# More projection steps ahead of the first head's scores, a pair of heads loaded in one round, and tiles of the mixture loaded two ahead

## The chip, the cores and the metric

The kernel runs on one NeuronCore of a Trainium2 chip. Its engines are TensorE (PE in the profile; PEld is its weight load), VectorE (DVE), ScalarE (ACT), GpSimd (POOL) and SyncE (SP). SP computes nothing here; it issues nearly all DMAs. The metric is the device time of one execution in microseconds (us). A kernel is run several times and the median is given; one further execution is recorded by the hardware profiler.

## The reference

One layer of an encoder, applied with the same weights to two token sets: A with 1024 tokens and B with 512, 1024 channels each. Cut to what matters:

```python
h = rms_norm(x, pre_w)
cols = h @ w_in                                  # about 10,800 columns
m_qk, m_v, m_o, m_z, m_i, m_f, a_qkv, a_z, gate = split(cols)
# branch A, bidirectional mLSTM, 4 heads x 256: q and k by a short conv + SiLU;
# per direction  h_t = (C_t q_t) / max(|n_t . q_t|, 1), gates from m_i and m_f
y_m = headnorm(h_fwd + h_bwd) * sigmoid(m_o) * silu(m_z)
# branch B, attention in 3 groups (window, dilation) = (128,1), (512,4), (2048,16),
# 8 heads x 64 each; the three outputs are mixed by their softmax denominators
o_g = softmax_unnormalised(q_g k_g^T + bias_g) v_g,  with row max m_g and denominator d_g
w_g = exp(m_g - max_g m_g)
y_a = (sum_g w_g o_g) / (sum_g w_g d_g) * silu(a_z)
merged = sigmoid(gate_0) * (y_m @ w_proj_m) + sigmoid(gate_1) * (y_a @ w_proj_a)
out = x + rms_norm(merged @ w_out, post_w)
```

All of it is float32. A dense product is made of three matmuls on a high and a low part of each operand (`mm3`, L190 to L196: high x high, high x low, low x high).

## The kernel before

**The first half** of the span projects the values of both token sets and then the remaining columns of A (`unit_pair`), ending with A's merge gates. **The second half**, from about 1056 us on, is what the change touches. It runs A's mLSTM, A's attention, B's mLSTM, B's attention and the closing products, in this order. Beside each of these stages TensorE is fed with *projection steps*: the projection of B's columns, and later the products with `w_proj_m`, `w_proj_a` and `w_out`.

**Steps and units.** `Fill` holds a list of units. A unit of B's projection makes 128 columns for 512 tokens; it is 8 steps, one for each 128 input channels, and a step is one `mm3`, three matmuls of 128x512. A unit needs one weight tile of 128x1024 (512 KB). The tile is loaded into one of two raw buffers (`wraw`), and `split_w` makes a high part (ACT, L252) and a low part (DVE, L253) into one of three pairs `wh`, `wl` (five pairs from B's attention on). Two tiles are loaded and split before the second half begins. When a unit is begun, `Fill.weights` calls `load`, which has the tile two units further on split (four units further on from B's attention on), and so has its DMA issued if it hasn't been. So the DMA of the third tile stands in the program at the begin of the first unit, the fourth at the begin of the second, the fifth at the begin of the third; the fifth uses the raw buffer of the third.

**Rate.** `fill.stage(steps, shares)` sets how many steps go with one share: A's mLSTM has 210 steps for `lead + 64 + 2 + 4` shares. `fill(lead)` is called before anything of the first head is computed; each of 64 rounds (4 heads x 8 chunks x 2 directions) calls `fill(1/3)` two or three times between its products.

**The order.** In the second half the instructions of TensorE and of SP stand in the order of the program; those of ACT, DVE and POOL are ordered at build time by a scheduler with a timing model. Each of these engines executes its own list in order, so an instruction that waits holds all behind it. SP's DMAs use eight semaphores in turn: a DMA is issued once the one eight before it has landed.

**The start of A's mLSTM** (`mlstm`). SP issues Q and K of the first head, the gate rows `rw`, then V0a and V0b, then whatever `fill(lead)` asks for. `prepare(0)` then computes the scores of the first head (L892) and turns K (L901), with a `fill(1/3)` after each of six parts; `front` builds the decayed scores of a round (`rm`, POOL L924, from `rw`), and `core` makes the products `num` and `kv`.

**B's attention** (`attend`, `attention`, `att_load`). Twelve pairs of heads, four tiles for each pair; a tile goes through `products` (`lg`, L1387), `softmax` (DVE L1399, ACT L1403), `turn` (`pt`, L1410, and its copy `pts`, L1413) and `output` (`o`, L1422), one stage a round, with one share of steps before `output`. At the second tile of a pair the loads of the next pair are queued: for the pair 1, twelve loads of 64 rows of 2 KB (Q and V1a) and two of the bias. `spread(r)` sets how many of the queued loads `tick` issues in a round: the queue's length divided by r, rounded up. `need` issues what is left when the pair begins. In the same rounds SP also loads the weight tiles `wraw<-w_pm`, and rows of `ym_a` (`ymr`, `sraw`) for the product with `w_proj_m`, which ACT splits at L1603.

**The mixtures** (`combine`). For each 128 tokens a tile `cs` of three loads (`og`, 528 bytes a row and pair of heads) is weighed (L1522 to L1533), mixed (L1541), added (L1547) and turned. There are two `cs` tiles. A's mixture runs as a generator beside B's mLSTM (`slow`, a part in each half round); B's runs after B's attention, beside steps of the closing products. `final` makes the closing product with `w_out`, in slots, and writes the result; its DVE instructions are L1711, L1716 and L1719.

Of the kernel before, what the change touches and what calls it, by code (L numbers as in the profile page):

```python
# [175 lines left out]
class Net:  # L176
# [1255 lines left out]
    def attend(self, T, fill, steps, first, banks, outs, after=None, beside=None, at=()):  # L1432

        nc = self.nc
        self.lag = 3 if T.n > 4 else 2
        with ExitStack() as st:
            ps = self.pool(st, "at_ps" + T.name, 2, "right", PSUM)
            sb = self.pool(st, "at" + T.name, 2, "right")  # L1440
            shape = {"lg": [P, 2, 256], "pt": [P, 4, P], "o": [P, 4, P]}
            make = lambda b: ps.tile(shape[b], F32, name=b, bufs=1 if b == "o" and T.n <= 4 else 2)
            spare = {b: make(b) for b in banks}
            self.bank = lambda b: spare.pop(b) if b in spare else make(b)
            bias = self.bias
            self.ot = Rot(self, [sb.tile([P, OW], F32, name=f"ot{i}", bufs=1) for i in range(outs)])
            tiles = []
            fill.stage(steps, 12 * T.n)

            self.xo_end = fill.done + steps  # L1450
            if T.n <= 4:
                self.third, self.fill = lambda: ps.tile([P, BLK], F32, name="dense3", bufs=1), fill

            def ready(u):
                nonlocal bias
                if u == 4 and T.n <= 4:
                    b = [x[F32] for x in bias.bufs]
                    bias = Rot(self, [b[i][:, c:c + 256].bitcast(F32R) for i in range(2) for c in (0, 256)])
                    self.xo_bufs.insert(0, ("stage", b[2:]))
                return self.attention(T, u, first if u == 0 else self.att_load(T, u), bias, sb, ps)  # L1460

            self.later = {}
            coming = ready(0)
            self.need(("table", 0))
            for i in range(12):
                now = coming
                for j, t in enumerate(now):
                    if j == 1:
                        if i < 11:
                            coming = ready(i + 1)  # L1470
                            self.spread(T.n - 1)
                        elif after:
                            after()
                            self.spread(T.n + 1)
                    self.tick()
                    if j == 0:
                        self.need(("att", i))
                    if j == 1:
                        self.need(("table", i))
                        self.later.pop(i, lambda: None)()  # L1480
                    tiles.append(t)
                    self.att_round(tiles, fill)
                    if len(tiles) in at:
                        next(beside, None)
            for _ in range(3):
                self.tick()
                tiles.append(None)
                self.att_round(tiles, fill)
            self.flush(lambda p: True)
            self.third = None  # L1490
            if T.n <= 4:
                self.xo_bufs = [x for x in self.xo_bufs if x[0] != "stage"]
# [10 lines left out]
    def combine(self, T, bank, cs, ys, sb, azs, slow):  # L1503

        nc = self.nc
        cs = [self.take(x, F32)[:, :12 * OW].rearrange("p (g a w) -> p g a w", g=3, a=4) for x in cs]
        ys = [self.take(x, F32) for x in ys]
        az_of = Rot(self, azs + [y[:, 1536:2048] for y in ys])  # L1510

        def load(t):
            for g in range(3):
                self.fetch(("og", T.S), cs[t % 2][:, g], T.og[g, :, t * P:(t + 1) * P].rearrange("h t w -> t h w"))

        by = lambda x: x.rearrange("p g (a b) -> p g a b", a=4)

        def weigh(t):
            c = cs[t % 2]
            w = sb.tile([P, 4, 8], F32, name="cw8", bufs=2)  # L1520
            den, mx = c[:, :, :, 128:130], c[:, :, :, 130:132]
            top = by(w[:, 3:4])[:, 0]  # L1522
            nc.vector.tensor_tensor(top, mx[:, 0], mx[:, 1], op=OP.max)
            nc.vector.tensor_tensor(top, top, mx[:, 2], op=OP.max)
            nc.vector.tensor_sub(by(w[:, :3]), mx, top[:, None].to_broadcast([P, 3, 4, 2]))
            nc.scalar.activation(w[:, :3], w[:, :3], AF.Exp)
            wd = sb.tile([P, 3, 8], F32, name="wd8", bufs=2)
            nc.vector.tensor_tensor(by(wd), by(w[:, :3]), den, op=OP.mult)
            nc.vector.tensor_add(wd[:, 0], wd[:, 0], wd[:, 1])
            nc.vector.tensor_add(wd[:, 0], wd[:, 0], wd[:, 2])  # L1530
            nc.vector.reciprocal(wd[:, 1], wd[:, 0])

            nc.vector.scalar_tensor_tensor(w[:, :3], w[:, :3], 0.5, wd[:, 1][:, None, :].to_broadcast([P, 3, 8]), op0=OP.mult,  # L1533
                                           op1=OP.mult)
            return w[:, :3]

        def mix(t, w):
            c = cs[t % 2]
            y = ys[t % 2][:, :1536].rearrange("p (g a w) -> p g a w", g=3, a=4)
            for g in range(3):  # L1540
                nc.vector.tensor_tensor(y[:, g].rearrange("p a (b e) -> p a b e", e=64),  # L1541
                                        c[:, g, :, :128].rearrange("p a (b e) -> p a b e", e=64),
                                        by(w)[:, g][:, :, :, None].to_broadcast([P, 4, 2, 64]), op=OP.mult)

        def add(t):
            y = ys[t % 2][:, :1536].rearrange("p (g x) -> p g x", g=3)
            nc.vector.tensor_add(y[:, 0], y[:, 0], y[:, 1])  # L1547
            nc.vector.tensor_add(y[:, 0], y[:, 0], y[:, 2])

        def turn(t, az):  # L1550
            p = bank()
            for ct in range(4):
                nc.tensor.transpose(p[:, ct], ys[t % 2][:, ct * P:(ct + 1) * P], self.ident)
            ya = az.rearrange("p (c s) -> p c s", c=4)
            nc.vector.tensor_mul(ya, p, ya)
            self.put(("ym", T.S, 4), T.ym[8:12, :, t * P:(t + 1) * P].rearrange("c p s -> p c s"), ya, az)

        load(0)
        yield
        az, w = {}, []  # L1560
        for t in range(T.n):
            az[t] = az_of()
            self.fetch(("az", T.S), az[t].rearrange("p (c s) -> p c s", c=4), T.az[:, :, t * P:(t + 1) * P].rearrange("c p s -> p c s"))
            if t + 1 < T.n:
                load(t + 1)
            for step in (lambda: w.append(weigh(t)), lambda: mix(t, w[t]), lambda: add(t)):
                with self.tc.issue_after(self.splits[0].ins), self.tc.issue_after(self.splits[1].ins):
                    step()
                if slow:
                    yield  # L1570
            if not slow:
                yield
                yield
            if t > 0:
                turn(t - 1, az[t - 1])
            yield
        yield
        if not slow:
            yield
        turn(T.n - 1, az[T.n - 1])  # L1580
        self.mixed.add(T)
        yield
# [172 lines left out]
STEPS = (210, 202, 164, 290, 86)  # L1755


def body(tc, a):
    N = Net(tc, a)
    nc = tc.nc  # L1760
    (x1, y1), (x2, y2) = a["runs"]
    with ExitStack() as st:
# [4 lines left out]
        A = Tokens(dram, 1024, a[x1], a[y1], "a")  # L1767
# [7 lines left out]
        with ExitStack() as s1:  # L1775
# [4 lines left out]
            with ExitStack() as sv:  # L1780
# [39 lines left out]
                def load(j, k):  # L1820
                    if k < 4:
                        hi, lo, w = HB[j][0][:, k], HB[j][1][:, k], N.prew[:, 4 * j + k:4 * j + k + 1]
                        nc.scalar.activation(hi, xb[j][:, k], AF.Copy, scale=w)
                        nc.vector.scalar_tensor_tensor(lo, xb[j][:, k], w, hi.bitcast(F32), op0=OP.mult, op1=OP.subtract)
                    elif k == 4:
                        for kh in range(2):
                            weights(1, kh)
                        scale(0)
                    else:
                        scale(1)  # L1830
                        inputs(0)
# [123 lines left out]
        with ExitStack() as s1:  # L1955
# [14 lines left out]
            fill = Fill(N, units)  # L1970
# [21 lines left out]
            with ExitStack() as s2:  # L1992
# [2 lines left out]
                sraw = sp.tile([P, BLK + 2], F32R, name="sraw")  # L1995
                N.sg, N.sraw = Rot(N, [sraw[:, :BLK]]), sraw.bitcast(F32)
                head = N.ml_load(A, 0)
                N.mlstm(A, fill, STEPS[0], head, ("a", "num", "kv"), 4,
                        hold("qkv", lambda: N.att_first(A)))
                with ExitStack() as s3:  # L2000
                    lanes = N.lanes_short(B, N.pool(s3, "lane2", 1, "right"), lambda: N.bank("o").rearrange("p a b -> p (a b)"))
# [96 lines left out]
```

## Time and profile before

| what | value |
|---|---|
| median of 3 runs | 2278.14 us (2277.72 to 2280.95) |
| the profiled execution | 2278.09 us, of which the span of the profile 2276.3 us |
| busy share of the span: PE, PEld, DVE, ACT, POOL | 98%, 86%, 64%, 48%, 27% |
| DMA, mean over the span | 187 GB/s, 425.05 MB |
| mean granted TensorE clock | 0.995 |

The span runs from the first to the last instruction of the program in the profile; the time of the execution is 1.8 us longer. Idle time of an engine is given with what ended it. A row of the timeline has the start, the duration, the engine and line, the tiles (out<-in), the shape and count, and in brackets the engine's idle time just before and its releaser. A row of the table by stretches has the stretch, its length, the busy time of PE, PEld, DVE, ACT and POOL with their counts, then the granted clock of TensorE, the busy share of the DMA engines, and GB/s.

### The profile page before, as it was taken

Reading aid. Unit: us, or ns where it says so; the run is one execution under the profiler, and the core shown is the slowest. Engines: PE = TensorE matmul, PEld = TensorE weight load, DVE = VectorE, ACT = ScalarE, POOL = GpSimd, SP = SyncE. Lnnn points to the kernel's source line nnn. Section 1 sums busy time; section 2 is a strip of 40 time slices with the busy share of each in tenths; the row PEclk is TensorE's granted clock in tenths of the full one; section 3 lists DMA queues with packets and bytes.
Section 4 is the critical chain, followed back from the end, with each engine's and each line's share of the span. In section 5 each row is a group of like instructions: output and inputs, shape, how many; then the busy total and the mean of one; then the engine's idle time right before and its main releaser. Section 6 shows DMA issues by size and latency. Waiting matters only on the chain. (4 is left out here: it accounts for less than half of the span.)

```text
span 2276.3 us, 35152 instructions
## 1 busy us (share of the span) xinstructions
PE 2235.5 (98%) x12210; PEld 1951.7 (86%) x12210; DVE 1467.8 (64%) x2777; ACT 1100.5 (48%) x2255; POOL 623.6 (27%) x801
## 2 busy tenths in 40 slices
PE   9999999999999999999999999999999999999998
PEld 9999998888887888887888889989888878888787
DVE  5587556767899655643787776675477744556563
ACT  7444223434444433334677766676644354544332
POOL 1000023333333322222567640001033321311311
PEclk9999999999999999999999999999999999999999
DMA  9556435555332223424666559988788888787673
GB/s 355 192 138 143 117 113 194 196 193 195 118 111 101 95 82 109 146 97 159 242 214 218 157 164 250 237 234 216 203 240 264 250 259 221 192 261 208 219 248 116
DMA packets 253627, 425.05 MB, mean 187 GB/s; under 512 B 26209, under 2 KB 150753, under 8 KB 252681
## 3 DMA queue, kind: packets, MB, share of 16 engines
q1 hardware_dynamic: 249848, 410.20, 58.7%
q10 hardware_dynamic: 3600, 12.59, 1.4%
q8 instruction: 97, 1.59, 0.3%
q14 instruction: 82, 0.66, 0.1%
HBM read 302.72 MB, written 128.37 MB: 189 GB/s over the span
## 5 line engine op out<-in xcount | busy, mean ns | idle before, releaser
L194 PE MATMUL dense<-H,wh 128*128 128x512 f32 x672 | 280.5, 417 | 0.0
L196 PE MATMUL dense<-H,wl 128*128 128x512 f32 x672 | 265.6, 395 | 0.5 <-DVE wl L253 0.5
L195 PE MATMUL dense<-H,wh 128*128 128x512 f32 x672 | 264.5, 394 | 0.0
L196 PE MATMUL d<-Hh,phla 128*128 128x512 f32 x608 | 237.4, 390 | 2.2 <-DVE phla L538 2.2
L194 PE MATMUL d<-Hh,phla 128*128 128x512 f32 x608 | 236.9, 390 | 0.0
L195 PE MATMUL d<-Hl,phla 128*128 128x512 f32 x608 | 236.8, 390 | 0.0
L195 PE MATMUL d<-vlo,Hh 128*128 128x322 f32 x704 | 220.4, 313 | 0.8 <-DVE vlo L384 0.8
L196 PE MATMUL d<-vhi,Hl 128*128 128x322 f32 x704 | 220.3, 313 | 0.0
L194 PE MATMUL d<-vhi,Hh 128*128 128x322 f32 x704 | 220.3, 313 | 0.0
L253 DVE TENSOR_TENSOR wl<-wraw,wh 128x1024 fp32r<-128x1024 f32 x109 | 137.0, 1257 | 89.8 <-ACT wh L252 87.7
L556 POOL TENSOR_TENSOR psum_w<-pw_raw 128x512 f32<-128x512 f32 x38 | 57.5, 1512 | 445.8 <-DMA pw_raw<-w_in 422.1
L1399 DVE CUSTOM_DVE_ANT_0 ls<-lg,bias 128x256 f32<-128x256 f32 (+1 forms) x288 | 93.7, 362 | 132.7 <-PE lg L1387 68.2
L194 PE MATMUL d<-Hh,phlb 128*128 128x512 f32 x456 | 177.6, 390 | 0.0
L196 PE MATMUL d<-Hh,phlb 128*128 128x512 f32 x456 | 177.6, 389 | 0.0
L195 PE MATMUL d<-Hl,phlb 128*128 128x512 f32 x456 | 177.6, 389 | 0.0
L1403 ACT ACTIVATE ls<-ls,nm 128x256 f32<-128x256 f32 (+1 forms) x288 | 129.9, 453 | 79.6 <-DVE nm L1401 63.1
L252 ACT ACTIVATE wh<-wraw 128x1024 fp32r<-128x1024 f32 x110 | 116.0, 1054 | 85.1 <-DMA wraw<-w_pm 32.8
L196 PEld LDWEIGHTS dense<-H,wl 128*128 128x128 f32 x672 | 126.7, 189 | 29.7 <-DVE wl L253 0.9
L195 PEld LDWEIGHTS dense<-H,wh 128*128 128x128 f32 x672 | 127.8, 190 | 13.6
L194 PEld LDWEIGHTS dense<-H,wh 128*128 128x128 f32 x672 | 127.4, 190 | 13.5
L196 PEld LDWEIGHTS d<-Hh,phla 128*128 128x128 f32 x608 | 114.1, 188 | 27.6 <-DVE phla L538 4.2
L195 PEld LDWEIGHTS d<-vlo,Hh 128*128 128x128 f32 x704 | 133.5, 190 | 1.5 <-DVE vlo L384 1.4
(556 smaller groups left out, 5722.2 us busy)
## 6 DMA issues: line engine op xcount, KB each, us to landing
pw_raw<-w_in SPq DMA_DIRECT2D x76, 512.0 KB
wraw<-w_in SPq DMA_DIRECT2D x76, 512.0 KB
aqk_a<-pwk SPq DMA_DIRECT2D x48, 512.0 KB
aqk_b<-sw SPq DMA_DIRECT2D x48, 256.0 KB
wraw<-w_pm SPq DMA_DIRECT2D x24, 512.0 KB
wraw<-w_out SPq DMA_DIRECT2D x24, 512.0 KB
vb<-w_vp SPq DMA_DIRECT2D x16, 644.0 KB
va<-w_vp SPq DMA_DIRECT2D x14, 644.0 KB
```

The source lines that it names most:

```text
L194: nc.tensor.matmul(out, lh, rh, start=start, stop=False)
L195: nc.tensor.matmul(out, lh, rl, start=False, stop=False)
L196: nc.tensor.matmul(out, ll, rh, start=False, stop=stop)
L252: self.splits = (nc.scalar.activation(hi[:, :n], raw[:, :n], AF.Copy), on.tensor_sub(lo[:, :n], raw[:, :n], hi[:, :n].bitcast(F32)))
L253: on.tensor_sub(lo[:, :n], raw[:, :n], hi[:, :n].bitcast(F32)))
L556: self.nc.gpsimd.tensor_add(s[:, 0], ws[1][:, 0], ws[1][:, 1])
L1399: nc.vector.tensor_tensor_reduce(out=ls[:, hh], in0=ts["lg"][hh], in1=bt[:, hh], scale=1.0, scalar=NEG, op0=OP.add, op1=OP.max, accum_out= ...
L1403: nc.scalar.activation(ls[:, hh], ls[:, hh], AF.Exp, bias=nm[:, hh:hh + 1], accum_out=ot[:, 128 + hh:129 + hh])
```

## The change

Three edits. In A's mLSTM the shares ahead of the first head's scores go from 4 to 8. In B's attention, and only for the loads that are queued during the first pair, `spread` gets 1 in place of `T.n - 1` = 3. In `combine` the tile 1 is loaded together with the tile 0, and after that the tile t + 2 is loaded once tile t has been mixed, in place of tile t + 1 just before tile t is weighed.

```diff
@@ attend
                     if j == 1:
                         if i < 11:
                             coming = ready(i + 1)
-                            self.spread(T.n - 1)
+                            self.spread(T.n - 1 if i or T.n > 4 else 1)
@@ combine
         load(0)
+        load(1)
         yield
         az, w = {}, []
         for t in range(T.n):
             az[t] = az_of()
             self.fetch(("az", T.S), az[t].rearrange("p (c s) -> p c s", c=4), T.az[:, :, t * P:(t + 1) * P].rearrange("c p s -> p c s"))
-            if t + 1 < T.n:
-                load(t + 1)
-            for step in (lambda: w.append(weigh(t)), lambda: mix(t, w[t]), lambda: add(t)):
+            for i, step in enumerate((lambda: w.append(weigh(t)), lambda: mix(t, w[t]), lambda: add(t))):
                 with self.tc.issue_after(self.splits[0].ins), self.tc.issue_after(self.splits[1].ins):
                     step()
                 if slow:
                     yield
+                    if i == 1 and t + 2 < T.n:
+                        load(t + 2)
             if not slow:
                 yield
+                if t + 2 < T.n:
+                    load(t + 2)
                 yield
             if t > 0:
                 turn(t - 1, az[t - 1])
@@ body
-                N.mlstm(A, fill, STEPS[0], head, ("a", "num", "kv"), 4,
+                N.mlstm(A, fill, STEPS[0], head, ("a", "num", "kv"), 8,
                         hold("qkv", lambda: N.att_first(A)))
```

## The prediction

> **What bounds the kernel now.** I read the page first: its span, and the busy time of TensorE.
>
> ```profile
> span 2276.3 us, 35152 instructions
> PE 2235.5 (98%) x12210; PEld 1951.7 (86%) x12210; DVE 1467.8 (64%) x2777; ACT 1100.5 (48%) x2255; POOL 623.6 (27%) x801
> ```
>
> TensorE is the bound, and no edit takes work from it: the same steps and products run before and after. At most 2276.3 - 2235.5 = 40.8 us of idle time, and what TensorE loses to its clock, can be won. So I asked next for TensorE's waits (waiter, releaser, us in total, times, longest) and for the granted clock, in stretches laid over its drops.
>
> ```profile
> PE lg L1387 <- DMA sraw<-ym_a: 4.7, 1, 4.7
> PE a L892 <- DMA K<-qk_a: 3.7, 2, 2.3
> ...
> PE dense L194 <- DVE mg L1716: 2.4, 1, 2.4
> ```
>
> ```profile
> 1068.76:1072.17 3.41, 3.41 (x16) 3.22 (x15) 0.02 (x1) 2.06 (x5) 2.98 (x6) 0.50 1.08 362
> 1099.48:1102.89 3.41, 3.41 (x16) 3.12 (x15) 1.35 (x3) 0.80 (x2) 0.88 (x3) 0.50 1.07 384
> ...
> 1857.24:1864.06 6.82, 3.71 (x11) 3.07 (x12) 2.77 (x7) 3.54 (x8) 3.74 (x5) 0.50 1.06 329
> 2143.96:2147.37 3.41, 3.41 (x9) 2.64 (x8) 3.41 (x12) 0.00 (x0) 0.00 (x0) 0.50 0.59 203
> ```
>
> Each stretch begins during or just after a wait (or two close together) of 2.3 us or more, and the clock is 0.50 in it. Busy time at half clock is half lost: 1.7 us in each stretch of 3.41, 1.9 us in the longer one with its 3.71 busy. Three of the four waits behind these stretches stand where the edits are: first head, short attention's second pair, B's mixture.
>
> **First head: what goes.** Its rows in order of time, TensorE's first:
>
> ```profile
> 1065.62 0.49 PE L892 MATMUL a<-Q,K 128*128 128x128 f32 x2 [1.47 <-DMA K<-qk_a]
> 1068.37 0.46 PE L892 MATMUL a<-Q,K 128*128 128x128 f32 x2 [2.26 <-DMA K<-qk_a]
> ...
> 1079.75 0.50 PE L196 MATMUL dense<-H,wl 128*128 128x512 f32 x1 [0.49 <-DVE wl L253]
> 1091.13 0.39 PE L194 MATMUL num<-V0a,sch 128*128 128x258 f32 x1 [0.68 <-ACT X L990]
> 1098.19 0.39 PE L194 MATMUL num<-V0a,sch 128*128 128x258 f32 x1 [2.29 <-ACT X L990]
> ```
>
> The waits sum to 1.47 + 2.26 + 0.49 + 0.68 + 2.29 = 7.2 us; with two stretches at half clock (3.4) the start of this stage loses 10.6 us. With more steps ahead, the two waits for K go: it has landed by 1068.4.
>
> **First head: what comes.** Four shares at 210/74 steps are 11 steps; eight at 210/78 are 21.5, so 22. Steps need weight tiles, one per 8:
>
> ```profile
> 1056.50:1064.15 7.65, 7.65 (x34) 6.01 (x32) 5.08 (x8) 2.78 (x4) 0.44 (x8) 1.00 0.73 219
> 1060.00:1076.00 16.00, 12.27 (x65) 10.48 (x64) 3.12 (x7) 5.02 (x12) 4.26 (x10) 0.89 1.04 366
> ```
>
> ```profile
> 1068.71 11.34 SPq L210 DMA_DIRECT2D wraw<-w_in  x3
> 1077.38 1.06 ACT L252 ACTIVATE wh<-wraw 128x1024 fp32r<-128x1024 f32 x1 [0.22 <-DMA wraw<-w_in]
> 1078.47 1.22 DVE L253 TENSOR_TENSOR wl<-wraw,wh 128x1024 fp32r<-128x1024 f32 x1 [0.99 <-ACT wh L252]
> ```
>
> The 11 steps (33 matmuls; one of the 34 overlaps) took 7.65 us, 0.695 each. Two tiles are at hand, 16 steps, which end at 1056.5 + 11.1 = 1067.6. The third tile is issued behind Q, K, rw and V at 1068.71, while the DMA engines are full (share 1.04), and ACT, which waited for it, splits it at 1077.38. Before, steps 12 to 16 were spread between the parts of `prepare`, and the 17th met the tile with 0.49 us to wait. None of the DMAs ahead of the tile waits for TensorE, so it comes no sooner. After, TensorE stands from 1067.6 to 1077.38 + 1.06 = 1078.4, 10.8 us; it makes two matmuls and waits for the low part, until 1079.7, 0.8 us more; then it runs some 3.4 us at half clock, 1.7 lost, as after the longest wait above. That is 13.3 us against 10.6, if the three later waits go. I think they do:
>
> ```profile
> 1088.52 0.29 POOL L924 TENSOR_SCALAR_AFFINE_SELECT rm<-rw 128x128 f32<-128x128 f32 x1 [2.37 <-DMA rw<-rw_a]
> ```
>
> POOL waited 2.37 us for gate rows; ACT's `rm`, and X in its order, stand behind what this delays. SP's order and times stay until about 1083, since it waits for landings and splits, not for TensorE, while the rounds begin about 13 us later, so the rows are there. Net +2.7 us. Should the later waits stay: 0.7 + 2.3 + 1.7 = 4.7 more.
>
> **The rounds.** About 184 calls of a third of a share make 174 steps at the old rate and 165 at the new. Nine calls more pass without a step, 0.68 us of cover each, 6.1 us in all.
>
> ```profile
> 1100.00:1345.00 245.00, 238.48 (x1501) 212.56 (x1500) 194.45 (x422) 178.03 (x450) 170.99 (x288) 0.99 0.60 192
> ```
>
> TensorE idles 6.5 of these 245 us, DVE is busy for 79%: mostly the cover isn't needed. Between 0 and 6.1 I take a quarter, 1.5. **First edit: +4.2 us** (ends -10.6 and +13.5).
>
> **Second pair.** SP, then ACT, then TensorE:
>
> ```profile
> 1838.60 2.09 SPq L231 DMA_DIRECT2D V1a<-aqk_b  x3
> 1841.65 0.34 SPq L210 DMA_DIRECT2D wraw<-w_pm  x1
> ...
> 1844.04 0.33 SPq L210 DMA_DIRECT2D wraw<-w_pm  x1
> ...
> 1854.11 1.09 SPq L231 DMA_DIRECT2D V1a<-aqk_b  x2
> ```
>
> ```profile
> 1848.34 1.06 ACT L252 ACTIVATE wh<-wraw 128x1024 fp32r<-128x1024 f32 x1 [2.96 <-DMA wraw<-w_pm]
> ...
> 1851.74 1.06 ACT L252 ACTIVATE wh<-wraw 128x1024 fp32r<-128x1024 f32 x1 [0.83 <-DMA wraw<-w_pm]
> ...
> 1853.70 0.59 ACT L1413 ACTIVATE pts<-pt 128x512 f32<-128x512 f32 x1
> ```
>
> ```profile
> 1854.31 1.00 PE L1422 MATMUL o<-X,pts 128*128 128x64 f32 x8
> ...
> 1860.34 1.15 PE L1387 MATMUL lg<-V1a,Q 128*128 128x256 f32 x2 [4.74 <-DMA sraw<-ym_a]
> ```
>
> The releaser's name is that of the neighbour: the matmul reads V1a, whose last two parts were issued at 1854.11, one round before use. Issued with the first five, they land in time: 4.74 + 1.9 = 6.6 us go. But the nine loads that two later rounds issued (fourteen less five) now stand ahead of the tiles at 1841.65 and 1844.04, and of `ymr`. Each is 131 KB (64 rows of 2 KB, or 128 of 1 KB), 1.18 MB in all, and
>
> ```profile
> 1836.00:1860.00 24.00, 19.59 (x103) 16.56 (x101) 11.15 (x25) 13.57 (x30) 6.90 (x5) 0.94 1.01 276
> ```
>
> at 276 GB/s 4.3 us later. TensorE needs these weights only four units on; ACT, in its fixed order, waits for them now. If `pts` stays behind the second split it ends 4.3 us later, and `o`, which followed it by 0.02 us, waits all of that, with a stretch at half clock: 6.0 us, gain 0.6. If `pts` moves before the second split, it follows the first, which ends at 1848.3 + 4.3 + 1.1 = 1853.7, and the work that stood between the two, 1851.74 - 0.83 - 1849.4 = 1.5 us: it ends 0.6 later, at 1855.8, and `o` waits 1.5 us, too short for a clock drop (the wait of 1.47 above had none). The scheduler sees the tiles issued later and should place them later; I take 1.5. **Second edit: -5.1 us** (ends -6.6 and -0.6).
>
> **B's mixture.**
>
> ```profile
> 2122.45 1.61 SPq L231 DMA_DIRECT2D V0a<-og_b  x3
> ...
> 2124.72 2.51 SPq L210 DMA_DIRECT2D wraw<-w_out  x2
> ...
> 2134.25 1.60 SPq L231 DMA_DIRECT2D V1a<-og_b  x3
> ```
>
> ```profile
> 2131.05 1.06 ACT L252 ACTIVATE X<-wraw 128x1024 fp32r<-128x1024 f32 x1 [0.71 <-DMA wraw<-w_out]
> 2133.42 0.50 PE L195 MATMUL dense<-X,H 128*128 128x512 f32 x1 [0.53 <-DVE X L253]
> 2141.61 0.17 DVE L1523 TENSOR_TENSOR cw<-V1a 128x8 f32<-128x8 f32 x1 [2.34 <-DMA V1a<-og_b]
> 2143.41 0.50 PE L194 MATMUL dense<-wh,H 128*128 128x512 f32 x1 [2.38 <-DVE mg L1716]
> 2124.00:2131.50 7.50, 7.50 (x35) 6.21 (x34) 1.83 (x2) 2.83 (x5) 1.34 (x2) 1.00 0.99 334
> ```
>
> DVE waited 2.34 us for V1a, with `mg` queued behind it and TensorE waiting for `mg`: 2.38 + 1.7 go. But V1a's three loads (3 x 128 x 4 x 528 bytes, 0.81 MB) pass ahead of the tiles of `w_out`, which have no slack (0.71 on ACT, 0.53 on TensorE) and full DMA engines: 0.81 MB at 334 GB/s is 2.4 us on TensorE, and 1.7 for the clock, since TensorE then waits some 3 us in all (2.4 + 0.53) between 2132.5 and 2136. **Net 0.0** (ends -4.1, nothing delayed; +1.6, SP's issue of the three loads comes on top).
>
> **A's mixture.** Its tile 1 only changes places with `az`; later tiles are asked for about two half rounds earlier. TensorE idles 1.82 us in this stage:
>
> ```profile
> 1660.00:1830.00 170.00, 168.18 (x999) 147.10 (x998) 128.93 (x307) 76.76 (x147) 59.12 (x87) 1.00 0.81 252
> ```
>
> I take 0, between -1.8 and +1.8. New wait: SP's load of tile t + 2 waits for DVE's mixing of tile t; weight tiles stand behind it.
>
> **Sum:** 4.2 - 5.1 + 0 + 0 = -0.9 us on the profiled execution's 2278.09, 0.05 under the median shown: **2277.2 us**.
>
> **A rule that speaks otherwise.** The Trainium skill, "TensorE: Matmul & The Clock Gate", section "HAM oscillation — how this bites in real kernels", warns of idle gaps over about 3.4 us. The trace differs: waits of 2.26, 2.29 and 2.38 us were followed by clock 0.50. By the rule the first head's two drops would not count as won (3.4 us), the mixture's would count on neither side, and the sum would be -0.9 + 3.4 = +2.5 us, 2280.6.
>
> **Rivals.** *As meant*: the third tile comes in time, nothing is put back: -10.6 + 1.5 - 6.6 - 4.1 = -19.8, **2258.3**. The DMA share of 1.04 speaks against it. Chance 0.08.
> *Delayed loads stay off the path*: the lead starves (+2.7), the rounds lose nothing, pair and mixture win in full: -8.0, **2270.1**. For it: weights four units ahead. Chance 0.23.
> *Steps moved from where they cover to where they starve* (slower): the 13.3 us are not paid back, because the second head's loads fill the queue again (+4.7), and the nine bare calls cost 6.1: +13.5 - 5.1 = +8.4, **2286.5**. It decides once the first edit costs over 9.7 us. For it: the wait at 1098 came in a stretch with DMA share above 1. Chance 0.25.
> *The pair's edit only renames its wait* (ACT behind `w_pm`, gain 0.6): **2281.7**. Chance 0.10.
> The Trainium skill ("DMA: Bandwidth & Descriptors", section "Queues, rings and completion order") has each DMA engine take descriptors in ring order, which speaks for this rival. The trace agrees so far: V1a's parts, issued last, held TensorE last.
>
> **How the numbers follow.** Forecast 0.34 (its own range 2273.6 to 2282.7). A measurement of this kernel can tell about 0.2%, 4.6 us, from no change. Faster 0.08 + 0.23 = 0.31; same 0.34 + 0.10 = 0.44; slower 0.25. The range 2262 to 2288 takes in all but the first rival and the upper end of the third.
>
> **What would show it.** Right: a wait of `dense` for `wh` or `wl` of 9 to 11 us near 1068 in place of K's, no POOL wait for `rw` by the tenth round, `lg` on V1a without a wait, `o` waiting 1 to 2 us for `pts`, a wait of 2 to 3 us for `w_out`'s split, none of DVE for V1a. Wrong: the third tile split before 1070, or waits summing to more than 10 us in A's rounds.

## The result and the profile after

The changed kernel takes **2294.61 us** (median of 4 runs, 2289.5 to 2295.99), the kernel before 2278.9 beside it: a ratio of 1.0067, 95% interval 1.0053 to 1.008. It is slower by 0.67%, outside the predicted range and on the other side of the forecast.

The page of the kernel after has the same work and 17.9 us more span:

```profile
span 2294.2 us, 35149 instructions
PE 2238.8 (98%) x12210; PEld 1954.1 (85%) x12210; DVE 1469.9 (64%) x2777; ACT 1099.9 (48%) x2255; POOL 619.5 (27%) x801
```

TensorE idles 2294.2 - 2238.8 = 55.4 us (40.8 before). Its waits, the largest first (us in total, times, longest):

```profile
PE dense L194 <- ACT wh L252: 11.3, 1, 11.3
PE o L1422 <- ACT ot L1424: 6.8, 7, 1.6
PE dense L194 <- DVE H L1655: 3.9, 1, 3.9
PE num L194 <- DVE r L988: 2.9, 1, 2.9
```

(From L1556 on, lines of the kernel after are 3 higher than before: L1655 is L1652 before.) The waits that the edits aimed at, of `a` for K and of `lg` for V1a, are gone, and each edit has a new one in their place. Where in the span the time went, I read from the start of the same TensorE instruction in both traces. The marks are the first step of the second half, the first `lg` of A's attention, an `lg` in B's first pair, an `lg` in B's second pair, the last `lg` of B's attention, and the first and the last turned tile (`tp`) of B's mixture:

| mark | before | after | later by | stage before the mark longer by |
|---|---|---|---|---|
| second half | 1056.51 | 1055.58 | -0.9 | |
| A's attention | 1351.88 | 1358.60 | +6.7 | +7.7, A's mLSTM |
| B's first pair | 1834.87 | 1844.48 | +9.6 | +2.9, A's attention and B's mLSTM |
| B's second pair | 1879.89 | 1884.10 | +4.2 | **-5.4**, the second pair |
| last `lg` | 2101.81 | 2113.34 | +11.5 | +7.3, the rest of B's attention |
| first `tp` | 2156.85 | 2167.78 | +10.9 | -0.6 |
| last `tp` | 2188.29 | 2206.19 | +17.9 | +7.0, B's mixture |

Behind the last mark nothing changes. **A's mLSTM**, in rows of the timeline of the kernel after (SP, ACT, TensorE) and in the table by stretches:

```profile
1067.82 11.68 SPq L210 DMA_DIRECT2D wraw<-w_in  x3
1076.83 1.06 ACT L252 ACTIVATE wh<-wraw 128x1024 fp32r<-128x1024 f32 x1 [5.22 <-DMA wraw<-w_in]
1077.94 0.80 PE L194 MATMUL dense<-H,wh 128*128 128x512 f32 x1 [11.31 <-ACT wh L252]
1084.10 1.95 PE L892 MATMUL a<-Q,K 128*128 128x128 f32 x16
```

```profile
1071.42:1081.66 10.24, 3.69 (x8) 2.48 (x9) 3.14 (x3) 2.31 (x3) 0.62 (x1) 0.50 0.66 223
```

The third weight tile is still issued behind Q, K, `rw` and V, and TensorE stands 11.31 us for its split, then works 3.69 us at half clock. The scores of the first head no longer wait (no bracket), but they begin 18.5 us later than before (1065.62), of which the eleven more steps, at 0.695 us each, are 7.6.

**B's second pair**: `lg` has no wait any more, and `o` waits 1.14 us. The fourteen loads stand ahead of the tile of `w_pm` (1859.03):

```profile
1848.31 3.86 SPq L231 DMA_DIRECT2D V1a<-aqk_b  x4
...
1854.87 2.95 SPq L231 DMA_DIRECT2D V1a<-aqk_b  x4
1857.87 1.06 SPq L231 DMA_DIRECT2D bias<-erep  x2
1859.03 0.37 SPq L210 DMA_DIRECT2D wraw<-w_pm  x1
```

```profile
1877.22 1.10 PE L1422 MATMUL o<-X,pts 128*128 128x64 f32 x8 [1.14 <-ACT ot L1424]
1890.76 1.11 PE L1422 MATMUL o<-X,pts 128*128 128x64 f32 x8 [0.95 <-ACT ot L1424]
```

**B's mixture**, SP first, then ACT, DVE and TensorE:

```profile
2148.71 0.90 SPq L1748 DMA_DIRECT2D xo<-x_prompt  x2
2157.88 1.56 SPq L231 DMA_DIRECT2D V0a<-og_b  x3
2159.49 0.97 SPq L1748 DMA_DIRECT2D xo<-x_prompt  x2
...
2166.67 1.02 SPq L1748 DMA_DIRECT2D xo<-x_prompt  x2
2167.79 1.48 SPq L231 DMA_DIRECT2D V1a<-og_b  x3
...
2170.61 1.68 SPq L210 DMA_DIRECT2D wraw<-w_pm  x2
...
2179.82 0.90 SPq L231 DMA_DIRECT2D gab<-gt_b  x2
```

```profile
2177.09 1.06 ACT L252 ACTIVATE wh<-wraw 128x1024 fp32r<-128x1024 f32 x1 [7.28 <-DMA wraw<-w_pm]
...
2183.63 0.69 DVE L1655 SCALAR_TENSOR_TENSOR H<-gab,dense 128x512 f32<-128x512 f32 x1 [2.94 <-DMA gab<-gt_b]
...
2184.46 0.76 PE L194 MATMUL dense<-V0b,wh 128*128 128x512 f32 x1 [3.87 <-DVE H L1655]
```

SP issues nothing from 2149.6 to 2157.88: the load of tile 2 (`V0a`) stands there and waits for the mixing of tile 0. Two loads of `xo` stand behind it. Ahead of the next two (2166.67) SP stands 4.3 us more, until `y_prompt<-xo` has landed. Then come tile 3 (`V1a`) and the next tiles of `w_pm` (2170.61), whose split sets free the raw buffer that the DMA ahead of the gate rows `gab` waits for. DVE gets `gab` late, and TensorE waits for DVE's `H`. The same part of SP's list in the kernel before:

```profile
2137.03 2.29 SPq L1745 DMA_DIRECT2D xo<-x_prompt  x4
...
2146.35 1.56 SPq L231 DMA_DIRECT2D V0a<-og_b  x3
...
2153.78 1.64 SPq L210 DMA_DIRECT2D wraw<-w_pm  x2
...
2161.13 0.90 SPq L231 DMA_DIRECT2D gab<-gt_b  x2
...
2162.55 1.69 SPq L231 DMA_DIRECT2D V1a<-og_b  x3
```

Counted from the first `tp` of each kernel, tile 2 is issued 9.9 us ahead of it after and 10.5 ahead before: the earlier place in the list does not bring it earlier, since it must wait for the mixing either way. Tile 3 does come earlier, at the first `tp` in place of 5.7 us behind it, and now ahead of `w_pm`. The tiles of `w_pm` come 5.9 us later and `gab` 7.8. Before, TensorE had no wait between the first and the last `tp`; after, it has three: 1.00 us for DVE's `mg`, 3.87 for `H` and 1.29 for `cw`, DVE's weighing in the mixture.

### The profile page after: what moved, and what is told of

It is laid out like the page before. It is cut to its first block, busy times and chain, and to the rows that moved or that the text cites. A ratio compares the mean times of both kernels' runs of the same rounds, so it can differ in the third digit from the quotient of the medians.

```text
span 2294.2 us, 35149 instructions
## 1 busy us (share of the span) xinstructions
PE 2238.8 (98%) x12210; PEld 1954.1 (85%) x12210; DVE 1469.9 (64%) x2777; ACT 1099.9 (48%) x2255; POOL 619.5 (27%) x801
## 3 DMA queue, kind: packets, MB, share of 16 engines
q8 instruction: 97, 1.59, 0.3%
## 5 line engine op out<-in xcount | busy, mean ns | idle before, releaser
L194 PE MATMUL dense<-H,wh 128*128 128x512 f32 x672 | 281.3, 419 | 11.3 <-ACT wh L252 11.3
L252 ACT ACTIVATE wh<-wraw 128x1024 fp32r<-128x1024 f32 x110 | 115.9, 1054 | 98.2 <-DMA wraw<-w_pm 41.8
```

What stands on the lines that cost most here:

```text
L194: nc.tensor.matmul(out, lh, rh, start=start, stop=False)
L252: self.splits = (nc.scalar.activation(hi[:, :n], raw[:, :n], AF.Copy), on.tensor_sub(lo[:, :n], raw[:, :n], hi[:, :n].bitcast(F32)))
```

## The experiments

Each run is timed against the kernel before on the same chip. The ratio with its 95% interval is of the times; the profile is of one execution. The last six columns give by how many us each stretch between the marks above is longer (+) or shorter (-) in the profiled execution than in that of the kernel before: A's mLSTM; A's attention and B's mLSTM; second pair; rest of B's attention; up to the first `tp`; B's mixture.

| run | us | ratio | mLSTM | A att. | pair | rest | to tp | mix. |
|---|---|---|---|---|---|---|---|---|
| kernel after | 2294.61 | 1.0067 (1.0053 to 1.008) | +7.7 | +2.9 | -5.4 | +7.3 | -0.6 | +7.0 |
| e1, first edit | 2285.42 | 1.003 (1.0017 to 1.0043) | +6.9 | +2.6 | +1.0 | 0.0 | -2.3 | 0.0 |
| e2, second edit | 2273.91 | 0.9976 (0.9963 to 0.9988) | -1.8 | +1.8 | -5.9 | +4.6 | -1.8 | -0.1 |
| e3, third edit | 2284.99 | 1.004 (1.0026 to 1.0053) | -2.0 | +2.4 | +0.5 | -0.7 | -1.3 | +7.9 |
| e7, second and third | 2285.02 | 1.0028 (1.0016 to 1.004) | +0.2 | +0.3 | -5.6 | +4.8 | +1.0 | +7.1 |
| f1, 8 shares, tile ahead | 2273.96 | 0.9978 (0.9968 to 0.9989) | -4.9 | -0.2 | +1.1 | +3.4 | -2.5 | 0.0 |
| f2, 6 shares, tile ahead | 2275.67 | 0.9985 (0.9975 to 0.9994) | -1.6 | +0.5 | +1.2 | +1.9 | -1.9 | -0.1 |
| g4, 4 shares, tile ahead | 2274.79 | 0.9994 (0.998 to 1.0008) | -3.8 | +2.2 | +2.2 | +1.2 | -0.7 | 0.0 |
| f3, pair in two rounds | 2269.49 | 0.9961 (0.9946 to 0.9975) | -3.9 | +1.3 | -6.1 | +2.2 | -1.0 | 0.0 |
| f4, only tile 1 early | 2277.07 | 0.9994 (0.9984 to 1.0004) | +2.1 | -0.1 | -0.6 | -0.4 | -2.1 | 0.0 |
| g3, f4 and SP's wait | 2280.75 | 1.0019 (1.0005 to 1.0034) | -0.2 | +0.3 | +2.5 | -0.9 | -0.9 | +3.7 |
| h2, third edit, B only | 2284.07 | 1.0034 (1.002 to 1.0047) | -0.5 | +1.2 | +0.9 | +0.8 | -1.3 | +8.0 |
| g1, after, tile ahead | 2276.85 | 1.0004 (0.9993 to 1.0015) | -6.0 | -0.2 | -5.5 | +3.3 | -0.3 | +7.7 |
| g2, f1 + f3 + f4 | 2271.8 | 0.9973 (0.9961 to 0.9984) | -2.0 | +3.1 | -5.2 | +1.4 | -0.7 | 0.0 |
| h1, f1 + f3 | 2266.41 | 0.9963 (0.9949 to 0.9977) | -5.5 | 0.0 | -6.1 | +2.2 | +0.1 | 0.0 |

Read it by columns. The second pair gains 5.2 to 6.1 us wherever the second edit is in, and nowhere else. The mixture loses 7.0 to 8.0 wherever B's tiles t + 2 are asked for early. The seven runs whose edits begin behind A's mLSTM show -3.9 to +2.1 in that stage: that is how far one execution may be off there. Other stages are as uncertain: in the rest of B's attention the eight runs without the second edit show -0.9 to +3.4, and in A's attention and B's mLSTM e2 and f3, whose edits touch neither, show +1.8 and +1.3.

**One edit each.** Each run has one hunk of the diff shown above; e7 has the second and the third.

> Only the first edit: 8 shares of steps ahead of the first head's scores. Theory 'starvation in place': TensorE stands 10 to 12 us for the third weight tile's split near 1068, as in the kernel after, and loses 7 to 8 us net by the end of A's mLSTM; nothing behind that stage has to do with the number of steps in front. Time 2278.9 + 7.7 = about 2286.6, or 2290 with the 3.2 us that A's attention lost as well. Rival 'shift': with every later step brought forward by some ten, the steps, weight tiles and splits of all later stages meet the products at other places, and the later losses of the kernel after (3.2 in A's attention, 7.3 in B's attention, 6.5 in B's mixture) come with this edit alone: about 2303. Rival 'no cost': the starvation only takes the place of waits that stood there before, 2277 to 2281.

2285.42 against 2277.67, +7.75: in place, as the first theory has it. Nothing is lost in B's attention or in the mixture, so the shift of all later steps by eleven did no harm there in this run.

> Only the second edit: the loads of B's attention's second pair queued in one round. Theory 'won in place and kept': the wait of the second pair's logits for V1a goes, `o` waits 1 to 2 us for `pts`, and the rest of B's attention and its mixture run as before: 2278.9 - 6.1 = about 2272.8. Rival 'given back': the nine loads that stand ahead of the tiles of w_pm make ACT's splits and copies late in the next pairs, `o` waits for its copies for some 7 us in sum later in B's attention, as in the kernel after: about 2280.

Between the two: -3.8 us. The pair itself gains 5.9, and 4.6 come back in the rest of B's attention. Rows of this run (SP, ACT), and its total of `o`'s waits (1.1 before):

```profile
1846.76 0.33 SPq L210 DMA_DIRECT2D wraw<-w_pm  x1
...
1851.03 1.06 ACT L252 ACTIVATE wh<-wraw 128x1024 fp32r<-128x1024 f32 x1 [5.09 <-DMA wraw<-w_pm]
```

```profile
PE o L1422 <- ACT ot L1424: 5.2, 6, 1.5
```

This execution is 2.35 us ahead of the one before at the first pair, so the tile's DMA is issued 1846.76 - 1841.65 + 2.35 = 7.5 us later in the stage, and ACT's split begins 1851.03 - 1848.34 + 2.35 = 5.0 later.

> Only the third edit: the mixtures' tiles loaded two ahead. Theory 'the loss in the closing products belongs to it': DVE no longer waits 2.3 us for V1a, but the late load behind the mixing of tile t, and weights behind that load, make TensorE wait near the end of B's mixture (3.9 and 1.3 us in the kernel after): 2278.9 + 6.5 = about 2285. Rival 'it wins what it was made for': the 2.4 us wait of the closing product for DVE and a stretch at half clock go and nothing comes for them: 2275 to 2277. Rival 'put back by the weights' (the prediction's): w_out's tiles come 2.4 us later, net nothing, 2278 to 2280.

2284.99 against 2277.67: as the first theory says, all of it between the first and the last `tp` (+7.9).

> The second and the third edit without the first (4 shares ahead). The kernel after less this one is what the first edit costs with the other two in place. Theory 'starvation in place': 2294.6 - 7.7 to 10.9 = 2283.7 to 2287, and the losses in the rest of B's attention (7.3) and in B's mixture (6.5) are still there. Rival 'shift': those losses came with the first edit, so this kernel takes 2278.9 - 6.1 - 2 = about 2271. The separate changes of the runs with one edit add up to this one's within 2 us if the edits don't act on each other.

2285.02: the losses of both edits are there without the first. The separate edits' ratios add up to 1 - 0.0024 + 0.004 = 1.0016, this run's is 1.0028, its interval begins at 1.0016. Against the kernel before in each case, the kernel after is 15.7 us slower and this one 7.4: 8.4 us, rounded, is the first edit's price in company. The three edits measured alone add up to 7.75 - 3.8 + 7.3 = 11.3 of the 15.7 us; the other 4.4 are no more than the four intervals together leave open (about 3 us to each side in each).

**The third tile ahead.** One line, ahead of the loads of Q and K; f1 has 8 shares, f2 has 6, g4 has 4:

```diff
+                N.flush(lambda p: p[1][0] == "w")
                 head = N.ml_load(A, 0)
-                N.mlstm(A, fill, STEPS[0], head, ("a", "num", "kv"), 4,
+                N.mlstm(A, fill, STEPS[0], head, ("a", "num", "kv"), 8,
```

> The first edit alone (8 shares), and the DMA of the third weight tile moved ahead of the first head's Q and K, into the 8 us before 1056 in which the DMA engines of the kernel before were idle. Theory 'the late third tile is the loss': TensorE's wait of 11 us near 1068 goes; the fourth tile, which is needed from the 25th step on and is still issued behind V, makes TensorE wait some 3 to 5 us near 1074 instead. Time 2277 to 2281, against 2285.4 of the first edit alone. Rival 'the steps moved ahead are missed as cover in the rounds': the wait goes, but waits of about its size come in A's rounds, 2284 to 2288.

2273.96 against 2278.92, 3 us below the expected figures. The tile's DMA is issued with the two before it, and the 11.31 us are gone:

```profile
1038.59 8.12 SPq L210 DMA_DIRECT2D wraw<-w_in  x3
1055.64 0.80 SPq L231 DMA_DIRECT2D Q<-qk_a  x2
```

```profile
1076.57 0.50 PE L194 MATMUL dense<-H,wh 128*128 128x512 f32 x1 [0.88 <-ACT wh L252]
1077.83 0.50 PE L196 MATMUL dense<-H,wl 128*128 128x512 f32 x1 [0.53 <-DVE wl L253]
```

The fourth tile costs 1.4 us in place of the 3 to 5 expected. The late third tile was the loss: 0.30% slower without, 0.22% faster with it.

> 6 shares, which are 17 steps, with the third tile's DMA moved ahead in the same way; neither of the other edits. Theory 'the late third tile is the loss': the 17 steps end near 1068, when K has landed, the fourth tile comes before the 25th step is due, so neither K nor a tile makes TensorE wait: of the 10.6 us lost there before (7.2 of waits, two stretches at half clock), 5.4 (the waits for K and one stretch) to 10.6 are won: 2268 to 2273.5. Rival 'the waits only move': 2277 to 2280.

A miss: 2275.67, between the two theories' figures. Neither K nor a tile makes TensorE wait, but from the 251st `num` on (about half of the rounds) TensorE idles 9.4 us, where it idles 4.2 in the kernel before, most of it in the rounds of the last head:

```profile
1298.23 0.39 PE L194 MATMUL num<-V1a,sch 128*128 128x258 f32 x1 [1.09 <-ACT X L990]
1303.64 0.39 PE L194 MATMUL num<-V1a,sch 128*128 128x258 f32 x1 [1.19 <-ACT X L990]
...
1320.74 0.55 PE L194 MATMUL num<-V1a,sch 128*128 128x258 f32 x1 [2.72 <-DVE X L993]
```

> The kernel before (4 shares) with the third tile's DMA moved ahead. Theory 'steps and tile belong together': with 11 steps in front the third tile was never what TensorE waited for but for 0.5 us, the two waits for K and a stretch at half clock stay: 2275 to 2279. Rival 'the early tile alone is the gain, the number of steps in front does nothing': 2272 to 2274.5, as with 8 shares and the tile.

2274.79, between the two theories' figures; 0.9994, an interval across 1, so the tile alone can't be told from no change. In its trace the two waits for K stay (1.64 and 2.03 us, with half the clock behind them), as the first theory says. With 8 shares the tile took off 12.7 us, with 4 shares 2.1, which is within the noise: the tile is worth much only with the steps in front. Whether f1 beats g4 the intervals do not settle.

> The kernel after, with the third weight tile's DMA moved ahead of the first head's Q and K and nothing else. The first edit cost 7.75 us alone and, with the tile moved, won 5.0: the tile is worth 12.7 with 8 shares. Theory 'the losses add up by their places': 2294.6 - 12.7 = about 2282, with the second edit's and the third's losses still there. Rival 'in the whole kernel the starvation hid behind other waits': over 2288.

2276.85, as fast as the kernel before: one line takes off the 15.7 us, 3 more than the 12.7 from e1 to f1, which is within the intervals. The table shows where this execution differs: A's attention is not longer here (2.9 in the kernel after), and the rest of B's attention by 3.3 (7.3). In the kernel after A's attention has a wait of `lg` for V1b (0.42 us before, 1.59 after) with half the clock behind it, and e1 (+2.6) has two, of 0.89 for V1a and 0.60 for V1b, with the same drop; why they are longer with 8 shares and the late tile is not settled.

**The pair in two rounds** (2 in place of 1):

```diff
-                            self.spread(T.n - 1)
+                            self.spread(T.n - 1 if i or T.n > 4 else 2)
```

> The second edit with two rounds for the fourteen loads in place of one: the last parts of V1a and the bias come one round earlier than in the kernel before, but only seven loads stand ahead of the first tile of w_pm. Theory 'the loads ahead of w_pm cost what is given back': the wait for V1a goes as with one round, ACT's splits of w_pm come 2 us later and not 5, and `o` waits less than 2 us in sum in the rest of B's attention, against 4.0 with one round: 2269 to 2272.5. Rival 'TensorE catches up with ACT whatever the loads do': `o` waits as long as with one round, 2273 to 2275.

2269.49, within the first theory's figures, but its condition was not met: `o` still waits 3.1 us in the rest of B's attention, where it was to wait less than 2 (4.5 in e2). The first tile of `w_pm` is issued at 1840.98, behind seven loads, and V1a's last parts behind it:

```profile
1840.98 0.34 SPq L210 DMA_DIRECT2D wraw<-w_pm  x1
...
1844.68 2.66 SPq L231 DMA_DIRECT2D V1a<-aqk_b  x4
```

```profile
PE o L1422 <- ACT ot L1424: 3.5, 5, 1.0
```

The pair gains 6.1 and 2.2 come back, where 4.6 did in e2. That two rounds give back less than one is not shown clear of noise: the intervals of e2 and f3 overlap, and 2.2 is no more than runs without the second edit show in that stage (f1 has +3.4, with 3.2 us of `o`'s waits). Not all of the 9.4 us by the times is the edit's: 3.9 of the profile's gain lie in A's mLSTM, where this kernel has the same instructions in the same order as before.

**The mixture.** f4 has `load(1)` beside `load(0)` and asks for the later tiles where the kernel before does. g3 adds, at the place where the kernel after loads tile t + 2 of B, a load of one pair of heads of its third group:

```diff
+                if t + 2 < T.n:
+                    self.fetch(("og", T.S), cs[t % 2][:, 2, 0:1], T.og[2, 0:1, (t + 2) * P:(t + 3) * P].rearrange("h t w -> t h w"))
```

> Half of the third edit: tile 1 of each mixture is loaded together with tile 0, the later tiles where the kernel before has them, after the mixing of t and just before t + 1 is weighed. Theory 'the early request for tile t + 2 is the loss': SP doesn't stand in front of the loads of xo, w_pm and the gate rows waiting for DVE's mixing, so the waits of 4.2 us and the stretch at half clock behind it (7.9 us in sum between the first and the last of B's turned tiles) don't come, and DVE's wait for V1a is gone: 2274 to 2278. Rival 'tile 1 itself is the loss, its 0.81 MB delay the weights': as with the whole edit, 2283 to 2286.

0.9994, no measurable change, and nothing lost in the mixture. SP issues all four loads of `xo` before it stands for tile 2, which is issued 9.9 us ahead of the first `tp`, as in the kernel after:

```profile
2137.39 2.81 SPq L1746 DMA_DIRECT2D xo<-x_prompt  x4
...
2145.39 1.56 SPq L231 DMA_DIRECT2D V0a<-og_b  x3
```

> Half of the third edit as in the run with tile 1 loaded together with tile 0, and at the place where the kernel after loads tile t + 2 of B's mixture one small load: one pair of heads of the third group, a twelfth of the tile's bytes, which is loaded again with the rest later. SP so waits for DVE's mixing of tile t at the early place, and the bytes stay late. Theory 'SP's wait is the loss': xo's loads, w_pm and the gate rows stand behind it, and TensorE waits 4 us or more near the end of B's mixture: 2282 to 2286. Rival 'the bytes ahead of w_pm are the loss': 2276 to 2279.

In between: 1.0019 against f4's 0.9994, and +3.7 in the mixture against 0.0. The wait of the small load keeps SP, after `xo` at 2136.58, until 2146.99:

```profile
2136.58 0.90 SPq L1748 DMA_DIRECT2D xo<-x_prompt  x2
2146.99 0.33 SPq L231 DMA_DIRECT2D V0a<-og_b  x1
2147.36 0.91 SPq L1748 DMA_DIRECT2D xo<-x_prompt  x2
```

But the 3.7 us are not half of the same loss. TensorE waits only 0.90 us for `H` here (3.87 in the kernel after); it waits 0.99 for `mg` and 2.2, in two waits, for DVE's adds (L1548) ahead of `tp`, and there is no stretch at half clock. SP does not stand for `y_prompt<-xo` (0.2 us in place of 4.3), and the tiles of `w_pm` come 2.8 us later than before, not 5.9. The rest of tile 2 is itself 4 us later here than in f4, so that some of the 3.7 can be that. How much of the 7 to 8 us is SP's wait alone is not settled.

> The third edit for B's mixture alone; A's mixture as before. The whole edit cost 7.3 us; with SP's wait at the early place but eleven twelfths of the bytes late, and A's mixture nearly as before, 3.9. What makes up the other 3.4? Theory 'the bytes of B's tiles ahead of w_pm': this run costs as much as the whole edit, 2283 to 2286. Rival 'A's mixture, with a drop of the clock near 1665': this run costs 3 to 4 us less, 2279.5 to 2282.

2284.07 against 2275.8, +8.0 in the mixture: A's mixture has no part in it. That asking early for tiles 2 and 3 of B costs it is shown by f4 against h2. Besides SP's first stand for tile 2, two things are in h2 and the kernel after and not in g3: the bytes of tile 3 go ahead of `w_pm`, and SP stands for `y_prompt`. It wasn't tried with the bytes early and SP free.

**Together.**

> 8 shares with the third tile moved ahead, the second pair's loads in two rounds, tile 1 of each mixture together with tile 0 and the later ones as before. Theory 'each is worth what it was worth alone': -5.0, -9.4 and -1.9 against the kernel before, 16 us in all: about 2262. Part of the second's 9.4 and of the first's was in stages that these edits don't touch (4 us each way), so 2260 to 2268. Rival 'the gains meet the same later waits (o for ACT in B's attention)': 2268 to 2273.

2271.8, where the rival had it. The pair's gain is there; A's attention lost 3.1 (in it a half-clock stretch) and A's mLSTM gained only 2.0. (The 5.5 us that the next expectation puts in B's mLSTM lie in the end of A's mLSTM and in A's attention.)

> 8 shares with the third tile moved ahead, and the second pair's loads in two rounds; the mixtures as before. The two took 5.0 and 9.4 us off when alone, and 5.1 together with tile 1 of the mixtures loaded early, where B's mLSTM lost 5.5 us by waits and two drops of the clock. Theory 'gains that stand in their own stages add up, and the rest is the lot of short waits that make the clock drop or not': -5.0 in A's mLSTM (profiled -6.7), -6 at the second pair, so -11 to -13: 2264 to 2267. Rival 'the gains meet a common later limit': no better than the pair alone, 2268 to 2272.

2266.41 against 2275.8. The time lies in the expected range, but the kernel before was fast beside it: the gain is 9.4 us, not 11 to 13. In the profile the two edits gain 5.5 and 6.1 in their own stages, and 2.2 are given back. Its ratio, 0.9963, is no better than f3's 0.9961, as the rival has it; the intervals can't tell them apart, so neither theory is shown. Its profile has a single stretch at half clock between 1060 and 2260 us, the kernel after eight. Both beat the kernel before and the kernel after.

## Why the prediction was wrong

In the profile 17.9 us came where -0.9 was forecast. By its steps:

**Starvation: right.** 10.8 + 0.8 + 1.7 = 13.3 was forecast; 11.31 and half of 3.69 is 13.2. That the sums agree to 0.1 us is luck: the wait was 0.5 longer, and the 0.8 for the low part did not come as a wait.

**The waits that go: right, but what the rounds lose was too small.** Of the five waits that sum to 7.2 us none is left; the rounds have one of 0.30 us there. The reason given for the last two did not hold: POOL still waits for `rw`, 3.38 and 3.94 us ahead of two `qw`, and 1.58 and 1.91 at the ninth and tenth `rm`, and TensorE is not held by it. The table by stretches, from the first step to the 251st `num` and on to A's attention, before and then after:

```profile
1056.51:1211.15 154.64, 144.84 (x892) 128.19 (x890) 112.81 (x236) 104.49 (x255) 90.36 (x159) 0.98 0.66 223
1211.15:1351.88 140.73, 136.52 (x839) 120.07 (x837) 107.68 (x236) 99.83 (x252) 96.52 (x163) 0.99 0.61 189
```

```profile
1055.58:1217.99 162.41, 147.90 (x909) 131.25 (x908) 114.08 (x235) 105.14 (x255) 88.83 (x158) 0.96 0.64 216
1217.99:1358.60 140.61, 134.09 (x823) 119.23 (x822) 107.58 (x237) 98.84 (x252) 96.08 (x164) 0.98 0.62 185
```

In the first stretch 9.80 us of idle time became 14.51, of which 11.31 are the tile's: the others fell from 9.80 to 3.20. Of these 2.87 are a new wait near 1155, with a drop of the clock behind it. In the second stretch 4.21 became 6.52, and one drop became two. For the nine bare calls I had taken a quarter of 6.1, 1.5 us. The idle time there did grow with 8 shares in every trace: the nine kernels with 4 shares idle 4.2 to 5.0 us in this stretch, the six with 8 shares 6.4 to 7.7. The second drop does not belong to it: e1, f1, g1 and h1 have none in this stretch. That the bare calls are the reason is not shown; with 6 shares, where fewer calls are bare, it is 9.4. The whole edit cost 7.75 us alone. 4.2 were forecast, inside its ends, and inside the interval of e1, 3.9 to 9.8 us.

**The second pair: right where I looked.** -5.1 was forecast, -5.4 came, `o` waits 1.14 us in place of 1.5, ACT's first split is 6.0 us later in the stage (5.0 in e2) in place of 4.3. **What failed is that the price ends there.** I priced the late splits once, at the next `o`, and took the rest as covered, because TensorE needs these weights only four units on. But `o` waits for ACT's copies `ot`, and these stand behind ACT's splits in its fixed order in later rounds too: 7 waits, 6.8 us in all (2 waits, 1.1 us before), and a drop of the clock near 2054. In the trace three of the seven, 2.5 us by 1898, stand behind splits of weight tiles (L252). The other four, 4.4 us from 1975 on, with the longest and its drop, stand behind splits of the rows `ymr`, whose loads ACT had waited for; two of them are there before, at 0.34 and 0.73 us. So TensorE, about 5 us further on, comes too early to an ACT that waits for its loads; that the fourteen loads make those later rows late is not shown. Alone the edit gave back 4.6 of 5.9, with two rounds 2.2 of 6.1. *The pair's edit only renames its wait* had ACT as the next limit, but at the wrong place.

**B's mixture: the step that failed most.** The wait of DVE for V1a went, `w_out`'s split made TensorE wait 1.27 and 0.77 us with a drop behind it, and up to the first `tp` the sum was -0.6 against 0.0: right, as far as one execution tells (runs without the third edit show -2.5 to +0.1 there). Then 7.0 us were lost that no term had. The prediction did name the mechanism, "SP's load of tile t + 2 waits for DVE's mixing of tile t; weight tiles stand behind it", but for A's mixture, where it was given 0. For B's mixture only tile 1 was priced, and as bytes; f4 shows that moving tile 1 changes nothing measurable. The requests for tiles 2 and 3 had no term. They cost 7.0 to 8.0 us in five traces, and in each of these TensorE waits 3.9 to 4.5 us for `H`, behind `w_pm` and `gab`.

**A's attention and B's mLSTM**, +2.9, had no term; runs that don't touch these stages show up to +1.8.

The misses sum up: first edit 3.5, A's attention 2.9, pair -0.3, rest of B's attention 7.3, mixture 6.4, less 0.9 by which this execution was ahead at the start, 18.9 in all, which is 17.9 + 0.9 to 0.1.

Of what was to show it, the wait for `wh` (11.31, a little over its 9 to 11), `lg` without a wait, `o` (1.14), the split of `w_out` (2.0 in all) and DVE without a wait for V1a came as said. POOL's waits for `rw` were to go and did not. The slower rival, at 2286.5, had the right side by another way: it took the three later waits to stay (+4.7), and they went, and the nine bare calls to cost 6.1, of which 2.3 at most are seen. Its point of decision, a first edit over 9.7 us, was not reached. By times the first edit and the third, which was put at 0.0, cost about as much each (7.75 and 7.3), and the second won 3.8 in place of 5.1.

## What to carry to other kernels

A load that is moved up in the list but must wait for compute need not come any earlier; it holds what is issued behind it on the same engine. Price that wait for everything behind it, not only the load's bytes. Steps put in front of a stage to cover a wait need their own inputs in front as well; here one line that loads the third tile into a time in which the DMA engines were idle (share 0.00 from 1048 to 1056 in the kernel before) turned a loss of 7.75 us into a gain of 5. And a gain on the bound engine must be followed until the mark where the next engine, here ACT behind its splits and their loads, sets the pace.

## What the runs showed of the hardware

The granted clock goes by a fixed grid of 3.4133 us. In all sixteen traces the half-clock stretches begin whole multiples of that length apart (in the kernel before, 9 windows from 1068.76 to 1099.48 and 315 to 2143.96), and what counts is TensorE's idle time **within one window** of the grid: between 1060 and 2260 us, all 59 windows with more than 1.9 us idle were followed by one at half clock, of 12 with 1.7 to 1.9 us 7 were, and of some 5,500 with less 16 were, nine of these in a window that was itself at half clock. The same wait can thus cost 1.7 us more or nothing more. `num` waits for X near 1288 in the kernel before (2.32 us) and in f3 (2.40 us), in the same order of instructions:

```profile
1289.74 0.39 PE L194 MATMUL num<-V1a,sch 128*128 128x258 f32 x1 [2.32 <-ACT X L990]
1287.21:1290.62 3.41, 1.09 (x6) 0.84 (x6) 2.15 (x4) 2.19 (x6) 2.37 (x4) 1.00 0.56 145
```

```profile
1287.86 0.39 PE L194 MATMUL num<-V1a,sch 128*128 128x258 f32 x1 [2.40 <-ACT X L990]
1283.80:1287.21 3.41, 1.65 (x9) 1.00 (x7) 2.76 (x7) 1.40 (x3) 3.26 (x5) 1.00 0.90 237
1287.21:1290.62 3.41, 2.76 (x17) 2.51 (x18) 2.35 (x6) 3.17 (x9) 1.34 (x4) 1.00 0.62 186
```

Before, the wait lies in one window (1.09 busy of 3.41), and a stretch at half clock begins at 1290.62. In f3 it is shared by two (1.65 and 2.76 busy; the first, with 1.76 us idle, is one of the 12 close cases), and the clock stays at 1.00. In A's mLSTM f3 has one drop where the kernel before has three; two drops are 3.4 of the -3.9 us in a stage that f3 doesn't touch.

The Trainium skill, "TensorE: Matmul & The Clock Gate", section "What's actually happening", gives a free-running window of 3413 ns. The traces agree with that: 3.413 us and a fixed grid. The Trainium skill, "TensorE: Matmul & The Clock Gate", section "HAM oscillation — how this bites in real kernels", warns of idle gaps over about 3.4 us. The traces differ: 1.9 us within one window were enough. The prediction booked 1.7 us for each wait above 2.3 us; by the grid such a wait can also cost no clock at all.
